# Four edits of an instruction order: the opening, the second half's x, the seam between the halves, the gate rows

## The chip, the cores and the metric

The kernel runs on one core of one Trainium2 chip. Five engines work side by side: TensorE (PE in the profile, its weight loads PEld), VectorE (DVE), ScalarE (ACT), GpSimd (POOL) and SyncE (SP), which issues nearly all DMAs. The metric is the device time of one execution in microseconds (us), median over runs; lower is better.

## The reference

One decoder block on x of 2048 tokens by 1024 channels, all in float32:

```python
mod = silu(c) @ w_ada + b_ada                       # shift, scale, gate: 1024 each
h = rms_norm(x, norm_w) * (1 + scale) + shift
a, b, g_conv, q, k, v, g_attn, m_conv, m_attn = split(h @ w_in)
u = silu(layer_norm(causal_conv31(a * sigmoid(b)))) * silu(g_conv)
y_conv = u @ w_conv_out
q, k = rope(rms_norm(q)), rope(rms_norm(k))         # 12 heads of 128
o = softmax_merge(dilated_window_attention(q, k, v) for 3 dilations) * silu(g_attn)
y = sigmoid(m_conv) * y_conv + sigmoid(m_attn) * (o @ w_attn_out)
out = x + gate * (y @ w_out)
```

## The kernel before

**Products.** Every projection is done with each operand split into a high and a low part (`_hi`, `_lo`; weights `sh`, `sl`), three matmuls for one. 2 × 2 blocks of tokens and channels are multiplied in the manner of Strassen, with seven block products (A11, A12, A21, A22 and sums S1 to S4 of blocks, against weights B11 to B22 and sums T1 to T4); `xs`, `s_d` and `h_d` hold such sums and scaled blocks of x. A slot is the time of one such block product on PE, some 12 matmuls of 128 × 128 by 128 × 512, and the whole program is laid out slot by slot.

**Order.** The tokens are done in two halves. In the first half come V of two pairs of heads (`plain_quads`, slots 0 to 15), four plain query and key jobs of eight slots (`qkv_plain`, slots 16 to 47), then a chain of `qkv_quad` jobs with the attention units between them, then the gates (`gate_quad`, `ag_quad`) and the convolution's inputs (`ab_quad`); the second half has the same without the plain jobs. `at_slot(s, f, where)` puts a step at a slot; `run_agenda` calls the steps of a slot in the order "enter", "load", "act", "pe", "vec", "act2", the product, "tail", "store". PE always runs in this written order. DVE, ACT, POOL and SP do so from the start of each half to a few slots behind its last attention unit; outside that, a scheduler orders them.

**DVE's spare work.** Steps of the convolution (`conv_todo`; tiles `ce`, `cq`, `ca`) and 32 steps that scale and sum the second half's x (`later_todo`; tiles `xl11`, `xl12`, `xl21`, `xl22`, `xs3`, in four groups k = 0 to 3; `run_later`, L1483) are handed out at the end of each slot by an allowance: `credit` grows by PACE (by stage) plus `rest`, falls by the estimated DVE time of the slot, and while it is over 0.35 another step is issued. A group's tiles are loaded (`later_load`) when group k − 2 is done. One DVE line, L210, records nearly all of these operations.

**The opening.** x of the first half (tiles `hf0` to `hf7`, second index for 512 tokens) is squared, its sums go through `xm` to `xrow` (L1022) and `xst` (L1028), the roots come back as `xr`, and `x_scale` (L1039, L1041) scales hf. `angle_steps` (L1109 to L1113) work out the rotary angles on spare_hi and spare_lo, ACT takes sines (L1111), `table_turn` (L1118 ff.) writes the tables. `mod` (L1059) is the conditioning for blocks A12 and A22.

**The gate rows.** In the second half's gates, 16 tiles `wg` of rows of w_ada (the part for `gate`) are loaded (L1587) and added to `gate_sum` on DVE (`gate_add`), then two bias rows, then `gate_sum` goes through PE.

**Banks.** A product's PSUM bank (`pav`, `pcv`, `pcab`, `pag_mc_d` and so on) must be emptied by ACT or DVE into spare_hi or spare_lo before PE can use it again; `ut` and `cq` are the first steps of a convolution block behind `pcab` and `paab`. `rwk` and `rsk` are the row of norms for keys and its spread.

## Time and profile before

| | |
|---|---|
| three runs | 2352.3, 2357.51, 2354.8 us; median 2354.8 |
| profiled execution | 2360.98 us; span 2358.4 us |
| granted TensorE clock in it | 0.993 |
| DMA | 445.76 MB, mean 189 GB/s |
| matmuls | 11438 |
| DVE, POOL instructions | 2792, 866 |

In the rows of the timeline the first number is the start in us from the span's start, the second the duration; then engine, line, operation, output <- inputs, and in brackets the idle time of that engine just before it and what ended it. Rows that follow each other overlap a little, since an engine begins an operation before the last has ended. Buffer numbers are left out of the names there; a name with a number belongs to the order of the program.

### The profile page before, as it was taken

To read this page: it belongs to the slowest core of one execution; us is meant where nothing else is said; L and a number is where in the kernel's file an instruction comes from. 1 tells how busy PE (TensorE), PEld (TensorE's weight loads), DVE (VectorE), ACT (ScalarE), POOL (GpSimd) and SP (SyncE) were. 2 spreads that over 40 slices of the span, in tenths; PEclk is the share of its full clock that TensorE was granted. 3 is DMA by queue.
4 is the path that set the end of the run, shared out by engine and by line. 5 is a ranking of instruction groups with operands and counts; after the bars stand their busy time and mean duration, and the time that the engine had idled before them with its cause. 6 is when DMAs were issued, how large, how long until landed. Compare 5 with 4: busy or idle time off the path is not lost.

```text
span 2358.4 us, 34462 instructions
## 1 busy us (share of the span) xinstructions
PE 2290.8 (97%) x11438; PEld 1868.6 (79%) x11438; DVE 1690.2 (72%) x2792; ACT 1120.8 (48%) x2291; POOL 1108.2 (47%) x866
## 2 busy tenths in 40 slices
PE   7999899999999999999999999999999999999999
PEld 4776688887878888787888887887888888888887
DVE  6668664566969789859746446799997957787544
ACT  5744455555644444654555545553444444332221
POOL 2345444545577789956433342445566630000221
PEclk9999999999999999999999999999999999999999
DMA  7567566665554455643666665655444579875553
GB/s 277 188 214 235 169 173 216 190 211 190 168 192 152 148 181 178 204 139 100 203 181 189 206 191 182 213 180 164 139 141 146 174 255 319 285 236 188 179 161 103
DMA packets 300942, 445.76 MB, mean 189 GB/s; under 512 B 28759, under 2 KB 132311, under 8 KB 300765
## 3 DMA queue, kind: packets, MB, share of 16 engines
q1 hardware_dynamic: 286648, 418.37, 55.8%
q10 hardware_dynamic: 14116, 25.20, 2.8%
q8 instruction: 90, 1.47, 0.3%
q14 instruction: 88, 0.71, 0.1%
HBM read 282.37 MB, written 161.09 MB: 188 GB/s over the span
## 4 chain that ended last, share of the span: by engine, by line
PE 50%; DVE 4%; DMA 2%; ACT 1%; issue 1%; POOL 0%; SPq 0%; ACTq 0%; DVEq 0%; POOLq 0%
PE yc L1710 8%; PE oa L1992 4%; PE ya L1710 4%; PE paab L345 3%; PE pak L345 3%; PE pav L345 3%; PE paq L345 2%; PE oc L1992 2%; PE pag_ma_d L345 2%; PE pcab L345 2%; PE pag_g_d L345 2%; PE po L945 2%; PE pcv L345 1%; DMA wg<-in_w_ada_dram 1%; PE pcq L345 1%; PE pck L345 1%
## 5 line engine op out<-in xcount | busy, mean ns | idle before, releaser
L282 POOL TENSOR_TENSOR slT<-wT,shT 128x512 fp32r<-128x512 f32 x172 | 232.8, 1354 | 283.9 <-ACT shT L281 270.6
L282 POOL TENSOR_TENSOR slB<-wB,shB 128x512 fp32r<-128x512 f32 x152 | 203.5, 1339 | 151.2 <-ACT shB L281 136.6
L281 ACT ACTIVATE shB<-wB 128x512 fp32r<-128x512 f32 x222 | 139.7, 630 | 167.5 <-issue 35.1
L282 POOL TENSOR_TENSOR slT<-wB,shT 128x512 fp32r<-128x512 f32 x98 | 131.8, 1350 | 148.1 <-ACT shT L281 120.6
L210 DVE SCALAR_TENSOR_TENSOR ce<-us,pair_taps,ce 128x512 f32<-128x512 f32 x240 | 180.9, 754 | 6.2
L210 DVE SCALAR_TENSOR_TENSOR ce<-ut,chan,ce 128x512 f32<-128x512 f32 x240 | 179.2, 747 | 0.5
L281 ACT ACTIVATE shT<-wT 128x512 fp32r<-128x512 f32 x176 | 110.4, 627 | 119.9 <-PE paab L345 21.2
L210 DVE SCALAR_TENSOR_TENSOR cq<-ut,chan,cq 128x512 f32<-128x512 f32 x208 | 155.2, 746 | 4.1 <-ACT cq L412 4.0
L210 DVE CUSTOM_DVE_ANT_0 sm<-ps,mask,rqq 128x256 f32<-128x256 f32 (+1 forms) x192 | 78.0, 443 | 93.0 <-PE ps L880 45.2
L276 POOL TENSOR_TENSOR wB<-wB,wB 128x512 f32<-128x512 f32 x80 | 111.2, 1391 | 47.2 <-DVE slB L210 44.1
L281 ACT ACTIVATE shT<-wB 128x512 fp32r<-128x512 f32 x120 | 75.2, 627 | 63.3 <-PE paab L345 30.7
L922 ACT ACTIVATE pT<-ptp 128x512 f32<-128x512 f32 (+2 forms) x84 | 44.8, 533 | 89.9 <-PE ptp L917 89.7
L139 POOL TENSOR_SCALAR stf<-stf 128x4 f32<-128x4 f32 x4 | 1.9, 473 | 179.9 <-DVE stf L1748 143.1
L945 PE MATMUL po<-v,pT 128*128 128x128 f32 x560 | 81.8, 277 | 3.0 <-ACT pT L922 2.8
L1920 ACT ACTIVATE yh<-yq 128x512 fp32r<-128x512 f32 x48 | 27.3, 623 | 120.4 <-POOL yq L1914 44.7
L945 PEld LDWEIGHTS po<-v,pT 128*128 128x128 f32 x560 | 75.1, 191 | 10.2 <-ACT pT L922 3.8
L210 DVE TENSOR_TENSOR slB<-wB,shB 128x512 fp32r<-128x512 f32 x70 | 54.9, 786 | 30.5 <-ACT shB L281 27.5
L902 ACT ACTIVATE sm<-sm,osb 128x256 f32<-128x256 f32 (+1 forms) x128 | 58.5, 463 | 4.2 <-DVE osb L210 4.2
L1911 POOL TENSOR_TENSOR ys<-yq 128x512 f32<-128x512 f32 x8 | 11.4, 1426 | 100.5 <-DMA yq<-y_d 88.8
L276 POOL TENSOR_TENSOR wT<-wB,wB 128x512 f32<-128x512 f32 x40 | 56.3, 1407 | 1.1
L917 PE MATMUL ptp<-ident,sm 128*128 128x128 f32 x332 | 52.3, 273 | 2.8 <-DVE stm L210 2.4
L622 POOL TENSOR_TENSOR slB_q<-wB_q,shB_q 128x512 fp32r<-128x512 f32 x16 | 29.5, 1846 | 54.3 <-ACT shB_q L621 49.7
(896 smaller groups left out, 7854.3 us busy)
## 6 DMA issues: line engine op xcount, KB each, us to landing
wB<-in_w_in_dram SPq DMA_DIRECT2D x262, 256.0 KB, 3.8
wT<-tT_d SPq DMA_DIRECT2D x136, 256.0 KB, 3.0
tT_d<-wB SPq DMA_DIRECT2D x102, 256.0 KB, 3.4
qk<-qk_d SPq DMA_DIRECT2D x96, 256.0 KB, 4.2
v_d<-vev SPq DMA_DIRECT2D x48, 256.0 KB, 3.4
qk_d<-spare_hi SPq DMA_DIRECT2D x48, 256.0 KB, 3.8
qk_d<-spare_lo SPq DMA_DIRECT2D x48, 256.0 KB, 4.1
v<-v_d SPq DMA_DIRECT2D x96, 128.0 KB, 3.9
```

Source lines behind the costliest of these rows:

```text
L210: return f(out, *args, **kw)
L276: nc.gpsimd.tensor_tensor(dst, x0, x1, op=ALU.subtract)
L281: nc.scalar.activation(h, q[name], AF.Copy)
L282: eng.tensor_tensor(l, q[name], h.bitcast(F32), op=ALU.subtract)
L345: nc.tensor.matmul(ps, x, y, start=(first and m == 0), stop=(last and m == 11), skip_group_check=True)
L622: nc.gpsimd.tensor_tensor(last[1], q[name], last[0].bitcast(F32), op=ALU.subtract)
L902: nc.scalar.activation(sm[:, a:z], sm[:, a:z], AF.Exp, scale=-1.0, bias=box["low"][i], accum_out=box["total"][i])
L917: nc.tensor.transpose(pt[:, c : c + P], box["sm"][:, c : c + P], ident)
L922: nc.scalar.activation(valid(pT), valid(pt), AF.Copy)
L945: nc.tensor.matmul(po[:, P * i : P * i + P], box["pT"][:, c : c + P], vt, start=(m == 0), stop=(m == count[i] - 1))
L1710: nc.tensor.matmul(pz, w, xx, start=(m == 0), stop=(m == len(terms) - 1))
L1992: nc.tensor.matmul(ps, y, w, start=(m == 0 and ps.name not in begun), stop=(m == 11 and not more), skip_group_check=True)
```

## The change

The diff is shown whole but for its headers.

```diff
-PACE, AFTER, AGAIN = (2.87, 3.15, 2.62, 2.85), (0.75, 0.1), 12
+PACE, AFTER, AGAIN = (2.87, 2.9, 2.62, 2.7), (1.0, 0.25), 12
...
     for k in range(4, KC):
-        at_slot(1, lambda k=k: x_scale(k, 0, pr), "act")
-    for s, count in ((0, 2), (1, 2), (2, 6)):
+        at_slot(2, lambda k=k: x_scale(k, 0, pr), "act")
+    for s, count in ((0, 2), (1, 1), (2, 5), (3, 2)):
         at_slot(s, lambda count=count: angle_steps(count))
...
         if k < 2 and later_todo[0][0] != k:
-            at_slot(s + 3, lambda: later_load(k + 2), "store")
-            later_from[k + 2] = s + 6
+            at_slot(s + 2, lambda: later_load(k + 2), "store")
+            later_from[k + 2] = s + 5
...
-        wa = aside["wg", i] = aside["gp"].tile([P, 512], F32, tag="wg", name=f"wg{i}")
+        wa = aside["wg", i] = aside["gp"].tile([P, 512], F32, tag="wg", name=f"wg{i}", bufs=2)
...
-        br = aside["gp"].tile([P, 512], F32, tag="wg", name=f"b_gate{i}")
+        br = aside["gp"].tile([P, 512], F32, tag="wg", name=f"b_gate{i}", bufs=2)
...
-        row = aside["gp"].tile([P, 512], F32, tag="wg", name=f"gate_out{i}")
+        row = aside["gp"].tile([P, 512], F32, tag="wg", name=f"gate_out{i}", bufs=2)
...
-    for i in range(2 * KC + 1):
-        if i:
-            at_slot(s + 2 * i, lambda i=i: gate_add(i - 1))
-        if i < 2 * KC:
-            at_slot(s + 2 * i, lambda i=i: gate_load(i))
+    for i in range(2 * KC):
+        at_slot(s + 2 * i, lambda i=i: gate_load(i), "load")
+        at_slot(s + 2 * i + 3, lambda i=i: gate_add(i))
...
-            kind, *job = jobs[i]
-            running[i] = kind(*job, columns[i][0])
+            running[i] = jobs[i][0](*jobs[i][1:], columns[i][0])
...
-        rest = AFTER[i >= half_jobs] if not waiting and s > busy_until[0] and stage % 2 else 0.0
-        credit = min(max(credit, -2.0) + PACE[stage] + rest - spent[0], 2.0)
+        rest = AFTER[i >= half_jobs] if not waiting and s > busy_until[0] and stage % 2 else 0.6 * (jobs[i][0] is qkv_plain)
+        credit = min(max(credit, -4.0) + PACE[stage] + rest - spent[0], 2.0)
```

In words: during plain query and key jobs the allowance grows by 0.6 per slot, its floor is −4 instead of −2, and the third and fourth group of x are loaded a slot sooner; the gate rows have two buffers, each row loaded at the start of its slot and added three slots later; in the opening four scalings go to slot 2 and the angle steps are dealt out anew. No instruction is added to PE or removed from it, and PE's order is the same.

On DVE, in the opening, the rows around the copy `xrow1` stood like this before (`hf2`, `hf3`: first 512 tokens):

```order
L1039 TENSOR_TENSOR hf2_0_176<-hf2_0_176,xr0_323 128x512 x2
L1039 TENSOR_TENSOR hf3_0_177<-hf3_0_177,xr0_323 128x512 x2
L1109 SCALAR_TENSOR_TENSOR spare_hi_169<-spare_lo_170,spare_hi_169 128x1024
L1109 SCALAR_TENSOR_TENSOR spare_hi_169<-spare_hi_169 128x1024
L1022 COPY xrow1_469<-xm1_415 128x128
L1028 TENSOR_SCALAR xst1_472<-xm1_415 128x4
L1109 SCALAR_TENSOR_TENSOR spare_hi_169<-spare_lo_170,spare_hi_169 128x1024
L1109 SCALAR_TENSOR_TENSOR spare_hi_169<-spare_hi_169 128x1024
L1110 TENSOR_SCALAR spare_hi_169<-spare_hi_169 128x1024
L1112 TENSOR_TENSOR spare_hi_169<-spare_hi_169 128x1024
L1113 TENSOR_SCALAR spare_hi_169<-spare_hi_169 128x1024
L1041 SCALAR_TENSOR_TENSOR hf0_1_178<-hf0_1_178,mod_140,xr1_495 128x512 x2
```
Here the scalings of hf2 and hf3 and two angle steps stand ahead of xrow1.

In the changed kernel the same stretch of DVE reads:

```order
L1109 SCALAR_TENSOR_TENSOR spare_hi_169<-spare_lo_170,spare_hi_169 128x1024
L1022 COPY xrow1_464<-xm1_411 128x128
L1028 TENSOR_SCALAR xst1_467<-xm1_411 128x4
L1039 TENSOR_TENSOR hf2_0_176<-hf2_0_176,xr0_323 128x512 x2
L1039 TENSOR_TENSOR hf3_0_177<-hf3_0_177,xr0_323 128x512 x2
L1109 SCALAR_TENSOR_TENSOR spare_hi_169<-spare_hi_169 128x1024
L1109 SCALAR_TENSOR_TENSOR spare_hi_169<-spare_lo_170,spare_hi_169 128x1024
L1109 SCALAR_TENSOR_TENSOR spare_hi_169<-spare_hi_169 128x1024
L1110 TENSOR_SCALAR spare_hi_169<-spare_hi_169 128x1024
L1041 SCALAR_TENSOR_TENSOR hf0_1_178<-hf0_1_178,mod_140,xr1_493 128x512 x2
L1085 SCALAR_TENSOR_TENSOR A21_lo_0_501<-hf0_1_178,mod_140,A21_hi_0_500 128x512
```
Now xrow1 and xst1 stand ahead of the four scalings; L1112 and L1113 follow behind four more rows, the last of them an A21_lo split.

On DVE, in the plain key jobs, ahead of the second use of `tmk` and `rwk`, the x steps stood like this before (`xl`, `xs3`: second half's x; the last digit is the group):

```order
L210 SCALAR_TENSOR_TENSOR xl212_1643<-xl212_1643,mod_140,rsx_1267 128x512
L210 TENSOR_TENSOR slB21_0_4096_1737<-wB21_0_4096_1652,shB21_0_4096_1736 128x512
L210 TENSOR_TENSOR S4_lo_0_1743<-s4_0_1684,S4_hi_0_1742 128x512
L210 SCALAR_TENSOR_TENSOR xl222_1645<-xl222_1645,mod_140,rsx_1267 128x512
L210 TENSOR_TENSOR S4_lo_0_1743<-s4_1_1705,S4_hi_0_1742 128x512
L210 TENSOR_TENSOR xs3_2_1809<-xl112_1639,xl212_1643 128x512
L210 SCALAR_TENSOR_TENSOR xl212_1643<-xl212_1643,edge_146,xl222_1645 128x512
L210 SCALAR_TENSOR_TENSOR xl112_1639<-xl212_1643,mod_140,xl112_1639 128x512
L210 SCALAR_TENSOR_TENSOR tmk0_1_00_1823<-spare_lo_170,hw_139,cos0_988 128x512
L210 SCALAR_TENSOR_TENSOR tmk0_1_01_1825<-spare_lo_170,hw_139,sin0_989 128x512
```
Group 2 is not finished where the rotation tmk begins.

In the changed kernel it reads there:

```order
L210 SCALAR_TENSOR_TENSOR xl112_1590<-xl212_1594,mod_140,xl112_1590 128x512
L210 TENSOR_TENSOR slB21_0_4096_1754<-wB21_0_4096_1657,shB21_0_4096_1753 128x512
L210 TENSOR_TENSOR S4_lo_0_1760<-s4_0_1697,S4_hi_0_1759 128x512
L210 SCALAR_TENSOR_TENSOR xl122_1592<-xl122_1592,mod_140,xl112_1590 128x512
L210 SCALAR_TENSOR_TENSOR xl113_1686<-xl113_1686,mod_140,rsx_1267 128x512
L210 SCALAR_TENSOR_TENSOR xl123_1688<-xl123_1688,mod_140,rsx_1267 128x512
L210 TENSOR_TENSOR S4_lo_0_1760<-s4_1_1721,S4_hi_0_1759 128x512
L210 SCALAR_TENSOR_TENSOR xl213_1690<-xl213_1690,mod_140,rsx_1267 128x512
L210 SCALAR_TENSOR_TENSOR xl223_1692<-xl223_1692,mod_140,rsx_1267 128x512
L210 TENSOR_TENSOR xs3_3_1824<-xl113_1686,xl213_1690 128x512
L210 SCALAR_TENSOR_TENSOR tmk0_1_00_1836<-spare_lo_170,hw_139,cos0_988 128x512
L210 SCALAR_TENSOR_TENSOR tmk0_1_01_1838<-spare_lo_170,hw_139,sin0_989 128x512
```
Group 2 is finished and five steps of group 3 are done ahead of tmk; over the whole stretch six more x steps stand ahead of the second rwk, and one fewer ahead of the third.

On DVE, at the seam between the halves, among the splits of the second half's first sums, the rows stood like this before (`ce`: convolution steps):

```order
L210 TENSOR_TENSOR S1_lo_1_9623<-landingS1_0_9512,S1_hi_1_9622 128x512
L210 SCALAR_TENSOR_TENSOR ce0_7_9230<-us0_7_9360,pair_taps_135,ce0_7_9230 128x512
L210 TENSOR_TENSOR S1_lo_1_9623<-landingS1_1_9514,S1_hi_1_9622 128x512
L210 TENSOR_TENSOR S1_lo_1_9623<-landingS1_2_9544,S1_hi_1_9622 128x512
L210 SCALAR_TENSOR_TENSOR ce0_7_9230<-us0_7_9360,pair_taps_135,ce0_7_9230 128x512
```
Two convolution steps stand between the S1 splits and the next.

In the changed kernel the same place reads:

```order
L210 TENSOR_TENSOR S2_lo_1_9537<-landingS2_2_9481,S2_hi_1_9536 128x512
L210 SCALAR_TENSOR_TENSOR ce0_7_9252<-us0_7_9386,pair_taps_135,ce0_7_9252 128x512 x3
L210 TENSOR_TENSOR S1_lo_1_9620<-landingS1_0_9511,S1_hi_1_9619 128x512
L210 TENSOR_TENSOR S1_lo_1_9620<-landingS1_1_9513,S1_hi_1_9619 128x512
L210 TENSOR_TENSOR S1_lo_1_9620<-landingS1_2_9542,S1_hi_1_9619 128x512
L210 TENSOR_TENSOR S3_lo_1_9683<-landingS3_0_9579,S3_hi_1_9682 128x512
L210 TENSOR_TENSOR S3_lo_1_9683<-landingS3_1_9581,S3_hi_1_9682 128x512
```
The two steps are gone from here; some twenty rows on, between the slT1 and slB22 splits, a run of five such steps has become one of seven.

On DVE, in the second half's gates, the adds of the rows stood like this around the eviction of `pcab` before:

```order
L210 SCALAR_TENSOR_TENSOR ce1_1_15844<-us1_1_15962,pair_taps_135,ce1_1_15844 128x512 x2
L210 SCALAR_TENSOR_TENSOR gate_sum_15996<-wg6_16301,sc_141,gate_sum_15996 128x512
L210 SCALAR_TENSOR_TENSOR ce1_1_15844<-us1_1_15962,pair_taps_135,ce1_1_15844 128x512 x3
L210 SCALAR_TENSOR_TENSOR gate_sum_15996<-wg7_16353,sc_141,gate_sum_15996 128x512
L210 SCALAR_TENSOR_TENSOR ce1_1_15844<-us1_1_15962,pair_taps_135,ce1_1_15844 128x512 x3
L210 TENSOR_TENSOR spare_lo_170<-spare_lo_170,pcab1_2_15757 128x512
L210 SCALAR_TENSOR_TENSOR gate_sum_15996<-wg8_16402,sc_141,gate_sum_15996 128x512
L210 SCALAR_TENSOR_TENSOR ce1_1_15844<-us1_1_15962,pair_taps_135,ce1_1_15844 128x512
L210 SCALAR_TENSOR_TENSOR ut1_2_15819<-spare_lo_170 128x2x256
L210 SCALAR_TENSOR_TENSOR ce1_1_15844<-us1_1_15962,pair_taps_135,ce1_1_15844 128x512
L210 SCALAR_TENSOR_TENSOR ut1_2_15819<-spare_lo_170,paab1_2_15689 128x2x256
L210 SCALAR_TENSOR_TENSOR ce1_1_15844<-us1_1_15962,pair_taps_135,ce1_1_15844 128x512
```
Eight row adds (wg0 to wg7) are done when pcab is evicted, with three convolution steps between two of them.

In the changed kernel it reads:

```order
L210 SCALAR_TENSOR_TENSOR gate_sum_15992<-wg12_16597,sc_141,gate_sum_15992 128x512
L210 SCALAR_TENSOR_TENSOR ce1_1_15864<-us1_1_15985,pair_taps_135,ce1_1_15864 128x512
L210 SCALAR_TENSOR_TENSOR gate_sum_15992<-wg13_16645,sc_141,gate_sum_15992 128x512
L210 SCALAR_TENSOR_TENSOR ce1_1_15864<-us1_1_15985,pair_taps_135,ce1_1_15864 128x512
L210 SCALAR_TENSOR_TENSOR gate_sum_15992<-wg14_16702,sc_141,gate_sum_15992 128x512
L210 SCALAR_TENSOR_TENSOR ce1_1_15864<-us1_1_15985,pair_taps_135,ce1_1_15864 128x512
L210 TENSOR_TENSOR spare_lo_170<-spare_lo_170,pcab1_2_15753 128x512
L210 SCALAR_TENSOR_TENSOR gate_sum_15992<-wg15_16749,sc_141,gate_sum_15992 128x512
L210 SCALAR_TENSOR_TENSOR ce1_1_15864<-us1_1_15985,pair_taps_135,ce1_1_15864 128x512
L210 TENSOR_TENSOR gate_sum_15992<-gate_sum_15992,b_gate0_16896 1x512
L210 SCALAR_TENSOR_TENSOR ut1_2_15819<-spare_lo_170 128x2x256
L210 SCALAR_TENSOR_TENSOR ut1_2_15819<-spare_lo_170,paab1_2_15684 128x2x256
```
Fifteen row adds are done when pcab is evicted, one convolution step stands between two of them, and a bias row stands ahead of ut.

## The prediction

> **What bounds the kernel now.** I read the page first (busy shares, the chain that ended last), then the table of stretches, then the timeline of the matmul engine (PE), stall by stall, and only then VectorE (DVE) around the four places that the change reaches.
>
> ```profile
> span 2358.4 us, 34462 instructions
> PE 2290.8 (97%) x11438; PEld 1868.6 (79%) x11438; DVE 1690.2 (72%) x2792; ACT 1120.8 (48%) x2291; POOL 1108.2 (47%) x866
> PE 50%; DVE 4%; DMA 2%; ACT 1%; issue 1%; POOL 0%; SPq 0%; ACTq 0%; DVEq 0%; POOLq 0%
> ```
>
> PE is the bound: 2358.4 − 2290.8 = 67.6 us of its span are idle, and a change that takes no matmul away can win only from these and from matmuls that run at half speed. In the stretches (length, busy time of PE, weight load, DVE, ACT, POOL with their counts, granted clock, DMA share, GB/s) the changed places differ from an undisturbed one, the last row:
>
> ```profile
> 0.00:50.00 50.00, 33.42 (x312) 22.07 (x316) 34.35 (x49) 22.16 (x34) 12.56 (x26) 0.93 0.81 302
> 200.00:250.00 50.00, 42.36 (x223) 31.84 (x223) 41.31 (x48) 18.63 (x30) 27.17 (x19) 0.93 0.62 201
> 1600.00:1650.00 50.00, 44.78 (x185) 36.15 (x184) 46.91 (x61) 19.00 (x33) 27.95 (x20) 0.93 0.52 169
> 1750.00:1800.00 50.00, 50.00 (x223) 41.38 (x222) 39.32 (x56) 23.72 (x40) 28.41 (x22) 1.00 0.48 158
> ```
>
> The stalls on PE at those places, the idle time in brackets with what ended it:
>
> ```profile
> 39.28 0.33 PE L1026 MATMUL xm<-ident,xrow 128*128 128x128 f32 x1 [2.99 <-DVE xrow L1022]
> 208.35 1.22 PE L737 MATMUL rsk<-rwk,pick 32*128 32x512 f32 x2 [3.18 <-DVE rwk L210]
> 260.24 0.50 PE L345 MATMUL pcv<-S_hi,shB 128*128 128x512 f32 x1 [1.07 <-DVE spare_hi L210]
> 265.89 1.19 PE L737 MATMUL rsk<-rwk,pick 32*128 32x512 f32 x2 [2.64 <-DVE rwk L210]
> 986.65 0.50 PE L345 MATMUL pav<-A_hi,shB 128*128 128x512 f32 x1 [2.98 <-ACT spare_hi L490]
> 1014.08 0.50 PE L345 MATMUL pcv<-S_hi,shB 128*128 128x512 f32 x1
> 1614.36 0.79 PE L345 MATMUL pag_mc_d<-S_hi,shT 128*128 128x512 f32 x1 [4.60 <-ACT spare_hi L360]
> 1614.95 0.63 PE L345 MATMUL pag_mc_d<-S_lo,shT 128*128 128x512 f32 x1
> 1642.54 0.50 PE L345 MATMUL pag_ma_d<-S_hi,shT 128*128 128x512 f32 x1 [0.61 <-ACT spare_lo L360]
> ```
>
> After the stalls of 2.64, 2.99, 3.18 and 4.60 us some ten matmuls run slow: they show 0.63 (row 1614.95) where an undisturbed one shows 0.40 (row 57.35 below), and ten times 0.23 is 2.3 us; read from the starts of the rows it is 1.7 to 2.9 each time. After the 2.98 at 986.65 none does. So a stall of this kind is worth its length plus up to 2.9. All that the change touches comes to about 25 us.
>
> PE's order does not change. DVE's does at four places, and only there: the two new PACE values, the new AFTER and the lower floor of the allowance move nothing in the first half's convolution, and little in the second's.
>
> **A, the opening.** xrow, which PE waits for (2.99), now stands on DVE ahead of four scalings of hf and one angle step; the angle steps L1112 and L1113 go behind the A21 splits.
>
> ```profile
> 34.16 2.47 DVE L1039 TENSOR_TENSOR hf<-hf,xr 128x512 f32<-128x512 f32 x4
> 38.95 0.28 DVE L1022 COPY xrow<-xm 128x128 f32<-128x128 f32 x1
> 45.22 1.23 DVE L1112 TENSOR_TENSOR spare_hi<-spare_hi 128x1024 f32<-128x1024 f32 x1 [2.22 <-ACT spare_hi L1111]
> 46.48 0.69 DVE L1113 TENSOR_SCALAR spare_hi<-spare_hi 128x1024 f32<-128x1024 f32 x1
> 53.32 2.03 ACT L1121 ACTIVATE ada_hi<-spare_hi 128x1024 f32<-128x1024 f32 x1
> 53.42 0.17 DVE L1059 TENSOR_TENSOR mod<-pt_ada,cols 128x8 f32<-128x8 f32 x1 [0.53 <-PE pt_ada L1056]
> 57.35 0.40 PE L345 MATMUL pC<-A_hi,shB_p 128*128 128x512 f32 x1
> ```
>
> xrow comes 2.47 us earlier, so the stall falls from 2.99 to about 0.5. But the four scalings are not gone; the same DVE work must be done before `mod`, on which A12, and so PE's slot from 57.35, depends. Between xrow and `mod` DVE idles for 2.22 + 0.53 = 2.75 us, so at most that can be won. The new order makes idle time of its own: DVE now stands at the foot of the chain PE → xrow → roots (about 1.4 with nothing ahead of it), and A21_lo waits for ACT, which has L1111 in front. I put these at 2.7, so `mod` stays near 53.3; ACT's table turn L1121 (2.03), which needs L1113, cannot start before that either, and A12_hi stands behind it. Bounds: −4.7 (stall 2.5 and the slow matmuls after it, if PE's lead lasts to 57.35) and +0.7 (L1113 later by its own length). I take 0, the end nearest to the row 57.35.
>
> **B, the second half's x.** With two of its groups loaded one slot sooner and 0.6 us per slot of extra allowance in the plain jobs, DVE does six more of these 32 steps before the second rwk, and one fewer before the third.
>
> ```profile
> L210 DVE SCALAR_TENSOR_TENSOR xl<-xl,mod,rsx x16: 739/746/1780, 138.6 to 224.1; 128x512 f32<-128x512 f32 x16
> 185.38 1.38 DVE L210 TENSOR_TENSOR S_lo<-s,S_hi 128x512 fp32r<-128x512 f32 x1 [1.94 <-ACT S_hi L193]
> 189.73 0.75 DVE L210 SCALAR_TENSOR_TENSOR xl<-xl,mod,xl 128x512 f32<-128x512 f32 x1 [0.47 <-DMA h_d<-xl]
> 207.63 0.67 DVE L210 TENSOR_TENSOR rwk<-pwk,edge 32x512 fp32r<-32x512 f32 x1
> 247.08 0.94 DVE L210 SCALAR_TENSOR_TENSOR xl<-xl,mod,xl 128x512 f32<-128x512 f32 x1
> ```
>
> Six steps by 0.70 (0.746 shown, less the overlap of neighbouring rows) are 4.2 us. DVE's idle time ahead of 207.63 that they can fill is 1.94 + 0.47 = 2.4. So rwk comes 4.2 − 2.4 = 1.8 later, and the stall of 3.18 becomes 5.0. The step at 247.08 (0.94 shown, 0.87 without the overlap) leaves the stretch in which DVE has no idle time before spare_hi (stall 1.07) and rwk (2.64): the first shrinks by 0.87, the second keeps its size because PE and DVE both come earlier. Net 1.8 − 0.9 = +0.9, plus 0.2 for a longer slow run: +1.1. The moved stores (h_d, s_d on SP's queue) have two slots to land and hide. Bounds: −0.9 (all six steps hidden) and +3.5 (none hidden, 4.2 + 0.2 − 0.9).
>
> **C, the seam between the halves.** Two convolution steps leave the stretch ahead of the add that feeds ACT's L490, and stand behind it in a run of seven instead of five.
>
> ```profile
> 982.18 1.27 DVE L210 TENSOR_TENSOR spare_hi<-spare_hi,pcg_g_d 128x512 f32<-128x512 f32 x2
> 1005.50 3.91 DVE L210 SCALAR_TENSOR_TENSOR ce<-us,pair_taps,ce 128x512 f32<-128x512 f32 x5
> 1012.94 1.08 DVE L210 TENSOR_TENSOR spare_hi<-spare_hi,pcv 128x512 f32<-128x512 f32 x1
> ```
>
> Two steps are 1.3 to 1.6 (3.91/5 = 0.78 each): the add at 982.18 and PE's 986.65 come about 1.3 earlier. The eviction at 1012.94 ends at 1014.02, and PE's pcv starts at 1014.08, so it has 0.1 us to spare. PE would reach it 1.3 earlier, and DVE does the same work before it: the 1.3 is given back there. Net +0.2; bounds −1.4 and +0.7.
>
> **D, the gate rows.** Sixteen rows of w_ada are loaded and added on DVE; one buffer forces load, add, load.
>
> ```profile
>   DMA wg<-in_w_ada_dram: 5.1, 7
> L210 DVE SCALAR_TENSOR_TENSOR gate_sum<-wg,sc,gate_sum x14: 739/1004/1839, 1582.0 to 1642.1; 128x512 f32<-128x512 f32 x14
> 1586.75 1.84 DVE L210 SCALAR_TENSOR_TENSOR gate_sum<-wg,sc,gate_sum 128x512 f32<-128x512 f32 x1
> 1586.75 1.29 POOL L282 TENSOR_TENSOR slT<-wT,shT 128x512 fp32r<-128x512 f32 x1 [2.08 <-ACT shT L281]
> 1601.33 0.33 SPq L1587 DMA_DIRECT2D wg<-in_w_ada_dram  x1
> 1604.58 0.75 DVE L210 SCALAR_TENSOR_TENSOR gate_sum<-wg,sc,gate_sum 128x512 f32<-128x512 f32 x1 [1.03 <-DMA wg<-in_w_ada_dram]
> 1607.49 0.68 DVE L210 TENSOR_TENSOR spare_lo<-spare_lo,pcab 128x512 f32<-128x512 f32 x1
> 1612.59 0.69 ACT L412 ACTIVATE cq<-ut,chan 128x512 f32<-128x512 f32 x1 [3.23 <-DVE ut L210]
> 1613.73 0.57 ACT L360 ACTIVATE spare_hi<-pag_mc_d 128x512 f32<-128x512 f32 x1
> ```
>
> Here the 4.60 us stall comes about: PE's bank waits for ACT's L360, which stands behind L412, which waits for ut, which waits for the pcab add. After the change 15 gate adds stand ahead of that add, not 8, and five convolution steps fewer: 7 × 0.75 − 5 × 0.75 = +1.5. The waits of 5.1 us mostly go, since a row has its own buffer. But the adds come in pairs, and a buffer is free only when its add is done: load to add takes 3.25 (1601.33 to 1604.58), and with 0.1 to issue and an add of 1.0 a buffer turns in 4.4 us, two rows per turn, while the DVE work between two pairs (two adds, two steps) is 3.0 to 3.5. So rows wg10 to wg15 wait about 1 us per pair, 3 in all. 1.5 − (4 of the 5.1 that lie ahead of the pcab add) + 3 = +0.5 to +1.7, and two bias rows and one step less behind it bring ut to +0.4. Behind 1613 the remaining seven adds are gone, so PE's next stall, 0.61 at 1642.54, is taken as gone. Sum +0.4 + 0.0 − 0.6, rounded up to 0 since the row loads now sit two at a time in front of weight loads on SP. Bounds: −6.5 (stall below 2.6 with no slow matmuls, plus the 0.6) and +5 (every one of the 7 extra adds takes 1.84 beside POOL, as in row 1586.75: 7 × 1.84 − 5 × 0.75 − 4 = +5.1).
>
> For that last price the trace has both values: 0.75 for a gate add alone, and 1.84 for one that begins together with POOL's slT. [...] Taken for every add, it gives the upper bound; half of them beside POOL would make the sum +2.
>
> **The sum.** A 0, B +1.1, C +0.2, D 0 = +1.3 on the profiled execution's span of 2358.4 (2360.98 with what lies around it). That execution is 6.2 us over the median of the three runs, 2354.8, and the forecast is made for such a median: 2354.8 + 1.3 = 2356.1.
>
> **Rivals.** R1, faster: the two buffers take DVE's waits on rows away in full, ut is ready 2.5 us sooner, the stall of 4.60 falls to about 2.1 and is not followed by slow matmuls: −2.5 − 2.9 − 0.6 = −6.0, 2348.8 with nothing else, 2350 with B and C. For it: 5.1 us of waits in seven places; against: 7 more adds ahead of ut. [...] R2, also faster: the opening's lead lasts, −4.7 and up to −6.0 with other parts hidden: 2350. Against it: DVE's 2.75 us of idle time are all there is. [...] R4: the moved steps fill idle time only, and nothing moves PE: 2354.8.
>
> **Chances.** Forecast 0.46, R4 0.10, R1 0.17, R2 0.12, R3 0.15. A difference under 0.2% (4.7 us) cannot be told from none here, so R1 and R2 count as faster at nine tenths, R3 as slower, and of the forecast's spread 0.01 and 0.02 reach over the bounds: faster 0.27, same 0.56, slower 0.17. The range 2348.5 to 2361 takes in R1 and R3 at their prices; the forecast's own is 2352 to 2359.
>
> **What would show it.** A: the stall at xm near 0.5, PE's pC slot still at about 57. B: the stall at the second rwk about 5.0. C: PE at pav earlier by 1.3, a new stall of about 1.5 at pcv some 28 us later. D: the stall at pag_mc_d within 1 us of 4.6, DVE waiting for wg in pairs among the last six rows. Wrong it would be if the slow matmuls vanish after 1610 or after 36, or if the stall before pag_mc_d passes 7 us.

## The result, and the profile after

The changed kernel is slower: 2366.6 us median (2362.93 to 2371.21) against 2357.02 (2352.3 to 2359.21), a ratio of 1.0043 with a 95% interval of 1.0029 to 1.0057, so +10 us (+6.8 to +13.4). The forecast was 2356.1 and no measurable difference; 2366.6 lies above the range. Measured again beside the kernels below, the same change gave 1.0046 (1.0032 to 1.0059).

The page of the changed kernel, and the same four stretches as before (length, busy time of PE, weight load, DVE, ACT, POOL with counts, clock, DMA share, GB/s):

```profile
span 2363.7 us, 34466 instructions
PE 2293.8 (97%) x11438; PEld 1869.7 (79%) x11438; DVE 1686.1 (71%) x2792; ACT 1120.4 (47%) x2291; POOL 1102.7 (47%) x866
0.00:50.00 50.00, 36.79 (x334) 23.35 (x334) 34.13 (x49) 22.67 (x36) 11.60 (x26) 0.93 0.77 295
200.00:250.00 50.00, 39.30 (x198) 29.12 (x197) 41.27 (x48) 18.33 (x30) 25.85 (x17) 0.93 0.56 175
1600.00:1650.00 50.00, 45.24 (x192) 36.93 (x192) 46.82 (x70) 20.24 (x35) 27.46 (x20) 0.97 0.54 169
1750.00:1800.00 50.00, 50.00 (x220) 41.04 (x219) 44.37 (x64) 24.18 (x42) 27.61 (x22) 1.00 0.49 153
```

PE idles 69.9 us, 2.3 more than in the profiled execution of before, and does the same matmuls. From 200 to 250 us it is busy 3.1 us less; in the first 50 us it is busy 3.4 us more, which turns out to be lost again by 64 us. The two profiled spans lie only 5.3 us apart, since the one shown of before was a long one: 2360.98 us where the median is 2357.

PE's stalls at the places of the prediction, from the timeline:

```profile
36.99 0.33 PE L1026 MATMUL xm<-ident,xrow 128*128 128x128 f32 x1 [0.48 <-DVE xrow L1022]
190.19 0.43 PE L688 MATMUL pssk<-sqk,sel 128*32 128x128 f32 x8 [1.49 <-ACT sqk L669]
201.67 0.50 PE L345 MATMUL pcq<-S_hi,slT 128*128 128x512 f32 x1 [1.40 <-DVE slT L210]
214.85 1.22 PE L737 MATMUL rsk<-rwk,pick 32*128 32x512 f32 x2 [5.42 <-DVE rwk L210]
992.30 0.50 PE L345 MATMUL pav<-A_hi,shB 128*128 128x512 f32 x1 [3.73 <-ACT spare_hi L490]
1020.43 0.50 PE L345 MATMUL pcv<-S_hi,shB 128*128 128x512 f32 x1 [0.64 <-DVE spare_hi L210]
1554.09 0.41 PE L966 MATMUL pta<-ident,osb 128*128 128x128 f32 x2 [1.16 <-DVE stm L210]
1621.76 0.64 PE L345 MATMUL pag_mc_d<-S_hi,shT 128*128 128x512 f32 x1 [4.76 <-ACT spare_hi L360]
```

The stall at xrow is gone as forecast, the one at rsk is 5.42 (forecast 5.0), and four stand where there was none: pssk, pcq, pcv (0.64, forecast about 1.5) and, in the second half's attention, pta.

### The profile page after: what moved, and what is told of

It reads as the page before. It is cut to its first block, busy times and chain, and to the rows that moved or that the text cites. A ratio compares the mean times of both kernels' runs of the same rounds, so it can differ in the third digit from the quotient of the medians.

```text
span 2363.7 us, 34466 instructions
## 1 busy us (share of the span) xinstructions
PE 2293.8 (97%) x11438; PEld 1869.7 (79%) x11438; DVE 1686.1 (71%) x2792; ACT 1120.4 (47%) x2291; POOL 1102.7 (47%) x866
## 4 chain that ended last, share of the span: by engine, by line
PE 51%; DVE 3%; DMA 2%; ACT 1%; issue 1%; POOL 0%; SPq 0%; ACTq 0%; DVEq 0%; POOLq 0%
PE yc L1707 8%; PE oa L1989 4%; PE ya L1707 4%; PE paab L345 3%; PE pak L345 3%; PE pav L345 3%; PE paq L345 2%; PE oc L1989 2%; PE pag_ma_d L345 2%; PE pcab L345 2%; PE po L945 2%; PE pag_g_d L345 1%; PE pcv L345 1%; PE pck L345 1%; PE pcq L345 1%; PE pag_mc_d L345 1%
## 5 line engine op out<-in xcount | busy, mean ns | idle before, releaser
L276 POOL TENSOR_TENSOR wB<-wB,wT 128x512 f32<-128x512 f32 x40 | 54.8, 1369 | 0.0
```

The lines of the kernel that those rows point to most:

```text
L276: nc.gpsimd.tensor_tensor(dst, x0, x1, op=ALU.subtract)
```

## The experiments

**How they are read.** PE runs the same matmuls in the same order in every kernel, so the time between two given matmuls can be compared kernel by kernel, whatever went before. The table is worked out from the starts of PE's rows; a stretch is named by its place in the profile of before. "With" are the kernels that hold the part in question as the change has it, "without" those that keep it as before; kernels that have it in another form are in neither column. Neither are, in the fourth row, g4_scale (56.41) and g1_x_actq (56.77), where DVE's order there is the new one though the opening is not. Each kernel counts with its one profiled execution.

| stretch, part | with: lowest to highest, mean | without: lowest to highest, mean | cost |
|---|---|---|---|
| 36 to 64, opening | 30.03 to 30.09, 30.05 (5 kernels) | 27.42 to 28.19, 27.92 (11) | +2.1 |
| 150 to 240, second half's x | 95.71 to 97.57, 96.53 (5) | 89.37 to 92.11, 91.27 (9) | +5.3 |
| 960 to 1030, PACE and AFTER | 71.28 to 74.12, 72.77 (6) | 69.85 to 74.46, 71.78 (14) | +1.0 |
| 1545 to 1600, opening's effect there | 54.96 to 56.70, 55.98 (5) | 54.96 to 56.27, 55.15 (13) | +0.8 |
| 1600 to 1660, gate rows | 58.05 to 59.47, 58.48 (5) | 54.05 to 60.04, 56.53 (13) | +2.0 |

The sum is some +11, and the change as a whole measured +10. In the first, second and last row the costs stand clear of the spread (in the last but for two kernels with the old rows, 54.05 and 60.04); in the third the two ranges cover nearly the same times, so that +1.0 is not shown by them. How far chance goes can be seen from 530 to 700 us, where the order is the same in all kernels: the time went from 164.98 to 170.67.

**Four parts, each alone on the kernel before.**

```diff
e1_open
-        at_slot(1, lambda k=k: x_scale(k, 0, pr), "act")
-    for s, count in ((0, 2), (1, 2), (2, 6)):
+        at_slot(2, lambda k=k: x_scale(k, 0, pr), "act")
+    for s, count in ((0, 2), (1, 1), (2, 5), (3, 2)):
e2_x
-            at_slot(s + 3, lambda: later_load(k + 2), "store")
-            later_from[k + 2] = s + 6
+            at_slot(s + 2, lambda: later_load(k + 2), "store")
+            later_from[k + 2] = s + 5
-        rest = AFTER[...] if ... else 0.0
+        rest = AFTER[...] if ... else 0.6 * (jobs[i][0] is qkv_plain)
-        credit = min(max(credit, -2.0) ...
+        credit = min(max(credit, -4.0) ...
e3_pace
-PACE, AFTER, AGAIN = (2.87, 3.15, 2.62, 2.85), (0.75, 0.1), 12
+PACE, AFTER, AGAIN = (2.87, 2.9, 2.62, 2.7), (1.0, 0.25), 12
e4_gate
-        wa = aside["wg", i] = aside["gp"].tile([P, 512], F32, tag="wg", name=f"wg{i}")
+        wa = aside["wg", i] = aside["gp"].tile([P, 512], F32, tag="wg", name=f"wg{i}", bufs=2)
...
-    for i in range(2 * KC + 1):
...
+    for i in range(2 * KC):
+        at_slot(s + 2 * i, lambda i=i: gate_load(i), "load")
+        at_slot(s + 2 * i + 3, lambda i=i: gate_add(i))
```

> The opening alone (four scalings to slot 2, angle steps dealt out anew). Theory 1 (angle steps L1112 and L1113 now run beside POOL's slB_p and take about 2 us more, mod comes 2 us later; besides, the moved scalings shift the scheduler's order near 1550 us): +2 to +3.5 us, L1112 near 2.3 us and L1113 near 1.7 us instead of 1.23 and 0.69. Theory 2 (the opening is even, the loss arises only when all parts are together): within 1 us of before.

Measured: ratio 0.9997 (0.9986 to 1.0008), so -3.3 to +1.9 us: in the total theory 2 holds and theory 1's +2 is not reached. The stretch from 36 to 64 us shows the loss, 30.04, as in all kernels with this opening, and L1112 and L1113 took 2.31 and 1.65, as theory 1 has it. The profiled execution won it back at the gate rows, by the shortest stretch of all kernels, 54.05, with a stall of 0.93 before pag_mc_d; DVE's order there is that of before, so this was chance, and it does not explain the median of twelve executions. Why the total shows no loss stays open.

> The second half's x alone (loads one slot sooner, 0.6 per slot more in the plain jobs, floor -4). Theory 1 (an in-place x sum waits for its store to land, about 4.8 us, and SP's queue passes the delay on to the loads of s): +4 to +5 us, DVE idle 4 to 5 us on a store h_d<-xl near 172 us, the stall before the second rsk 5 us or more. Theory 3 (only the six steps' own time counts, as forecast): +1.1 us, no wait on h_d over 1 us.

Measured: 1.0012 (1.0002 to 1.0023), stretch 95.71. DVE waited 3.96 us for a store h_d<-xl, and the stall at rsk was 5.85. Theory 1 holds on the places; in time the interval reaches from +0.5 to +5.4, which theory 3's +1.1 lies in as well, but its "no wait on h_d over 1 us" is out.

> PACE and AFTER alone (two convolution steps moved behind the seam). Theory 1 (without the two steps the S splits queue behind POOL for just as long, so nothing is won ahead of the seam and 0.6 us is lost at pcv): +1 to +1.5 us. Theory 3 (won ahead, given back behind): +0.2 us, the stall before pav under 2 us.

Measured: 1.0005 (0.9994 to 1.0016). The stall before pav is 3.65, where ten of the 14 kernels that keep the old order had 3.63 to 4.83 and four 2.91 to 2.98; so nothing was won ahead of the seam. At pcv 1.97 us stand where there was nothing. Too small for the total to tell.

> The gate rows alone (two buffers, each row added three slots after its load). Theory 1 (as forecast, ut hardly later, the stall before pag_mc_d about 4.7 us, the one of 0.6 us behind it gone): -2 to 0 us. Rival (two buffers take the waits away): -6 us, stall under 2.6 us. Rival (adds packed beside POOL): +5 us.

Measured: 1.0000 (0.9989 to 1.0011). The stall before pag_mc_d was 3.99, so the rival of -6 is out; +5 is out too. The stretch took 58.16, 1.6 over the mean of the old rows.

**The change with one part left out, and whole.** `f1_no_x`, `f2_no_open` and `f3_no_gate` are the change without the lines of e2_x, e1_open and e4_gate; `f4_all` is the change.

```diff
f4_all, all of the above; f1_no_x without e2_x; f2_no_open without e1_open; f3_no_gate without e4_gate
+            kind, *job = jobs[i]
+            running[i] = kind(*job, columns[i][0])
-            running[i] = jobs[i][0](*jobs[i][1:], columns[i][0])
```

> The change without its part for the second half's x (opening, PACE and AFTER, gate rows stay). Additive theory (the sum of the single parts, -0.7 + 1.2 + 0): about +0.5 us. Theory of the gate region (with the new gate order a delay from upstream is no longer taken up in the old stall near 1610 us): +2 to +4 us. Theory 1 (the x part carries nearly half of the loss): 4 to 5 us faster than the whole change.

Measured: 1.0019 (1.0007 to 1.0032), +4.5 us. Against 1.0046 for the whole, the x part is the largest single loss, some 6 us.

> The change without the new opening. Additive theory: about +4 us (2.8 + 1.2 + 0). Theory of the gate region: +5 to +7 us, with the stall before pag_mc_d at 4 us or more.

Measured: 1.0039 (1.0027 to 1.0051), +9.2 us (+6.4 to +12.0), more than both theories have; stall before pag_mc_d 4.03.

> The change with the old gate rows (one buffer, load and add in turn). Additive theory: about +3.3 us, as the whole change. Theory of the gate region: +1 to +3 us, clearly below the whole change, with the stall before pag_mc_d near 1 to 2.3 us as in the single parts with the old gate rows.

Measured: 1.0031 (1.0021 to 1.0041), +7.3 us, again more than both have; stall before pag_mc_d 2.09.

> The whole change again (its one line that only unpacks a job is left as before; the order is the same), on the same chip as the kernels that leave a part out. Additive theory: +3.3 us (0.14%). Theory of the gate region: +7 to +10 us, as in the first comparison.

Measured: 1.0046 (1.0032 to 1.0059). The sum of the stretches, +11, gives 1.0047. The +3.3 read from the four totals is out; each of those has an interval of ±2.6 us, their sum one of about ±5, and they were read too finely. That the parts add up is not refuted by it: stretch by stretch they cost alone about what they cost together. In the total the theory of the gate region, +7 to +10, came nearer, but its place does not show it: in the stretch of the gate rows the old order took 56.32 in f3_no_gate, with the delays of all other parts ahead of it, and 56.53 on average.

**The opening: where the steps stand.**

```diff
g4_scale
-        at_slot(1, lambda k=k: x_scale(k, 0, pr), "act")
+        at_slot(2, lambda k=k: x_scale(k, 0, pr), "act")
g2_open_fill
-    for k in range(4, KC):
-        at_slot(1, lambda k=k: x_scale(k, 0, pr), "act")
-    for s, count in ((0, 2), (1, 2), (2, 6)):
+    for s, count in ((0, 2), (1, 2), (2, 4)):
         at_slot(s, lambda count=count: angle_steps(count))
+    for k in range(4, KC):
+        at_slot(2, lambda k=k: x_scale(k, 0, pr))
+    at_slot(2, lambda: angle_steps(2))
```

> The opening with only the four scalings moved, the angle steps as before. Theory 1: the stall before xm near 0.5 us, L1112 and L1113 at 1.23 and 0.69 us, the stretch from 36 to 64 us at 27.5 to 28.2 us (no gain, since the work ahead of mod is the same, and no loss).

Measured in one execution: the stretch took 28.75, over the range expected and over the 27.42 to 28.19 of the old opening, L1112 and L1113 1.22 and 0.69. So the scalings alone gain nothing, and most of the loss belongs to the angle steps. Timelines, of the changed kernel (DVE, then POOL) and of g2_open_fill:

```profile
51.37 2.30 DVE L1112 TENSOR_TENSOR spare_hi<-spare_hi 128x1024 f32<-128x1024 f32 x1
53.71 1.66 DVE L1113 TENSOR_SCALAR spare_hi<-spare_hi 128x1024 f32<-128x1024 f32 x1
55.29 0.15 DVE L1059 TENSOR_TENSOR mod<-pt_ada,cols 128x8 f32<-128x8 f32 x1
51.27 3.54 POOL L327 TENSOR_TENSOR slB_p<-wB_p,shB_p 128x512 fp32r<-128x512 f32 x2 [12.59 <-ACT shB_p L326]
```

```profile
43.09 1.21 DVE L1112 TENSOR_TENSOR spare_hi<-spare_hi 128x1024 f32<-128x1024 f32 x1
44.34 0.69 DVE L1113 TENSOR_SCALAR spare_hi<-spare_hi 128x1024 f32<-128x1024 f32 x1
52.65 0.17 DVE L1059 TENSOR_TENSOR mod<-pt_ada,cols 128x8 f32<-128x8 f32 x1 [1.89 <-PE pt_ada L1056]
```

In the changed kernel both steps begin together with POOL's slB_p and take 1.07 and 0.97 us longer than at 45 us before; mod is 1.87 later than its 53.42. There `mod` waits for no PE, it follows L1113 at once; without the 2.04 us that the two steps lost it would stand at 53.25 (an estimate). In g2_open_fill POOL is idle beside them, its slB_p begins at 50.57, and they have their old lengths, 1.21 and 0.69.

> The opening in another order: the four scalings stand between L1110 and L1112, where DVE waited 2.2 us for ACT's sine, and the angle steps keep their slots. Theory 1 (the loss was L1112 and L1113 beside POOL): L1112 1.23 and L1113 0.69 us again, the stretch of PE products from 36 to 64 us (28.0 before, 30.05 with the new opening) falls to 27.3 to 28.0; time within 1 us of before or 1 us faster. Theory of DVE's idle time (filling 2.2 us wins it all): 26 us there, 2 us faster.

Measured: 0.9997 (0.9986 to 1.0009), stretch 26.26, below what theory 1 expected and near the 26 of the other theory, whose 2 us in the total did not come. PE's stall has moved from xrow (0.48) to xr (3.17), and the slow matmuls that follow the stall at xrow in the profile of before are missing. With the same opening two kernels below took 26.24 (h4_best) and 28.06 (i2_fill_load, with slow matmuls behind xr). So no gain is shown in the total; the 2.1 us of loss are gone.

**The gate rows: waiting or packing?**

```diff
g3_gate4, as e4_gate but
-bufs=2
+bufs=4
```

> The gate rows alone, with four buffers instead of two. If the 1.8 us lost with two buffers come from DVE waiting for rows: DVE's wait on wg under 1 us, the stall before pag_mc_d under 2 us, the stretch of products 1600 to 1660 us at 55 to 57 (56.7 on average with the old rows, 58.5 with two buffers). If they come from the seven more adds ahead of the pcab eviction: stall 4 us or more and 58 or more, waits or not.

Measured: 0.9994 (0.9982 to 1.0007). DVE's waits on rows, from the waits of DVE between 1570 and 1660 us, in the changed kernel and in g3_gate4 (total, times, longest):

```profile
DVE gate_sum L210 <- DMA wg<-in_w_ada_dram: 4.9, 7, 1.3
```

```profile
DVE gate_sum L210 <- DMA wg<-in_w_ada_dram: 0.9, 1, 0.9
```

The stretch falls to 56.57, that of the old rows, but the stall is 3.36, between the 0.93 to 2.40 of the old rows (the profile of before, 4.60, apart) and the 3.99 to 5.78 of two buffers. The other kernel with four buffers, h4_best below, has 57.83 and 3.38. So neither theory holds whole.

The traces show where the two differ. With four buffers all sixteen rows and both bias rows stand ahead of the pcab eviction, ten more than before, and yet it comes no later: counted from the same PE matmul (at 1561.66 in the profile of before) at 44.57 and 45.37 us, where the old rows had it at 43.34 to 44.83 (before, 45.82, apart) and two buffers at 46.48 to 48.27. DVE's idle time just before the row adds ahead of it was 1.0 to 1.2 us with four buffers, 2.1 to 3.7 with the old rows and 3.5 to 4.9 with two buffers. So with two buffers the eviction is late, by the waits and the seven more adds together. What is left with four buffers comes behind the eviction, from a ut step that took 1.71 instead of 0.68. The same happened in the profile of before; ut and POOL's slT there, and in e2_x, which has the old rows too:

```profile
1609.53 1.77 DVE L210 SCALAR_TENSOR_TENSOR ut<-spare_lo 128x512 f32<-128x512 f32 x1
1609.49 1.26 POOL L282 TENSOR_TENSOR slT<-wT,shT 128x512 fp32r<-128x512 f32 x1 [5.78 <-ACT shT L281]
```

```profile
1614.52 0.68 DVE L210 SCALAR_TENSOR_TENSOR ut<-spare_lo 128x512 f32<-128x512 f32 x1
1614.60 1.75 POOL L282 TENSOR_TENSOR slT<-wT,shT 128x512 fp32r<-128x512 f32 x1 [4.71 <-ACT shT L281]
```

In both, the one that begins first keeps its length (slT 1.26, ut 0.68), and the other takes longer: ut 1.77 for 0.68, slT 1.75 for 1.26. In the profile of before slT was first, by 0.04, and the eviction was 1.1 late; these two make the 4.60 of some 2.4.

**The x part: which half, and through which queue?** In the changed kernel, the timelines of DVE, ACT and SP's queue:

```profile
174.88 0.75 DVE L210 SCALAR_TENSOR_TENSOR xl<-xl,mod,xl 128x512 f32<-128x512 f32 x1 [4.80 <-DMA h_d<-xl]
186.84 0.63 ACT L193 ACTIVATE S_hi<-s 128x512 fp32r<-128x512 f32 x1 [5.15 <-DMA s<-s_d]
165.51 3.86 SPq L1442 DMA_DIRECT2D xl<-in_xt_dram  x4
169.46 0.85 SPq L1445 DMA_DIRECT2D h_d<-xl  x2
171.87 4.11 SPq L1445 DMA_DIRECT2D s_d<-xl  x3
176.07 1.86 SPq L271 DMA_DIRECT2D wB<-in_w_in_dram  x4
178.07 2.49 SPq L1442 DMA_DIRECT2D xl<-in_xt_dram  x4
180.67 0.37 SPq L1393 DMA_DIRECT2D s<-s_d  x1
```

An x step works in place on a tile whose store h_d is still under way. That store was issued at 169.46 or after, behind four x loads that themselves wait for older stores (1.8 us for an s_d). DVE stands for 4.80 us; the store s_d of the step's result stands on SP (the run from 171.87 takes 4.11); and behind it wait the weights wB and the loads of s (first half's S4), for which ACT idles 5.15. ACT's eviction and square come late, and PE waits at pssk. The transfers themselves are not slower: a load of s took 6.0 us from issue to landing in the kernel before, 5.0 to 5.9 in h2_x_load and h3_x_rest below, and 3.9 to 6.6 in e2_x and the changed kernel, as far as the traces have its landing. Each experiment on this has its first wB load, first s load, DVE's wait on h_d and its stretch in the table; in the kernel before they are 168.2, 173.4, 0.5 and 92.0.

| kernel | wB us | s us | DVE on h_d us | 150 to 240 |
|---|---|---|---|---|
| h2_x_load | 168.6 | 173.3 | 1.6 | 88.99 |
| h3_x_rest | 171.2 | 174.5 | 0 | 91.26 |
| e2_x | 173.2 | 178.0 | 4.0 | 95.71 |
| g1_x_actq | 168.7 | 182.2 | 0.2 | 99.76 |
| h1_x_sact | 173.2 | 179.6 | 4.0 | 97.61 |
| i1_x_searly | 174.6 | 177.5 | 5.4 | 97.58 |

```diff
g1_x_actq, as e2_x and
-        at_slot(slot_now[0] + 1, lambda: nc.sync.dma_start(dst, src), "store")
+        at_slot(slot_now[0] + 1, lambda: nc.scalar.dma_start(dst, src), "store")
h1_x_sact, as e2_x and
-        nc.sync.dma_start(parked[k], s4_d[k])
+        nc.scalar.dma_start(parked[k], s4_d[k])
h2_x_load, of e2_x the later_load and later_from lines alone
h3_x_rest, of e2_x the rest and credit lines alone
i1_x_searly, as e2_x and
-        at_slot(last_a21 - 1 + k, lambda k=k: s4_load(k), "load")
+        at_slot(last_a21 - 2 + k, lambda k=k: s4_load(k), "load")
```

> The x part alone, with the stores of the scaled x (h_d, s_d) issued on ACT's queue instead of SP's. Theory 1 (the delay comes from SP's queue in order: the store of xl12 stands behind others, DVE waits 4 to 5 us for it, and the loads of s stand behind the next store): DVE's wait on h_d falls under 1.5 us, ACT's wait on s under 2 us, the stretch of PE products that took 92.0 before and 95.7 with the x part (150 to 240 us) falls to 92.5 to 93.5. Theory 3 (the six steps' own time): stays at 95 or more with no wait on h_d.

Measured: 1.0021 (1.0006 to 1.0037). The wait on h_d went as expected, the time did not: now SP's x loads waited 13.6 us for the stores on the other queue, and s stood behind them. Theory 1, that the h_d wait is the cause by itself, falls.

> The x part alone, with only the four loads of s (the first half's S4, tile s from s4_d) issued on ACT's queue, so that they no longer stand behind the x loads and stores on SP's. If the order of SP's queue makes the x part slow: ACT's wait on s under 1.5 us, no PE stall over 0.5 us at pssk near 188 us, the stretch of PE products 150 to 240 us at 93 to 94.5 (96.5 on average with the x part, 91.6 without). If the transfers themselves are slow because eight others run at once: s still lands 5 us or more after its issue and ACT still waits 3 us or more, 95.5 or more.

Measured: 1.0021 (1.0010 to 1.0032). This did not take away what it meant to: the loads of s were issued no sooner, and ACT, whose queue they were on, stood 3.60 us in their place. Rows of SP's and ACT's queues in this kernel:

```profile
173.21 1.84 SPq L271 DMA_DIRECT2D wB<-in_w_in_dram  x4
179.55 0.34 ACTq L1393 DMA_DIRECT2D s<-s_d  x1
179.93 0.63 ACT L669 ACTIVATE sqk<-spare_lo 128x512 f32<-128x512 f32 x1 [3.60 <-DMA wB<-in_w_in_dram]
```

> Only the loads of the third and fourth x group one slot sooner, the allowance as before. If the bunch of loads and stores ahead of s is what costs: 92 to 93.5 in the stretch 150 to 240 us (the x steps hardly move). If the sooner loads alone do it: 95 or more.

Measured: 88.99, and 2350.35 us for one execution, below what either theory has. The sooner loads alone cost nothing.

> Only the larger allowance in the plain jobs and the lower floor, the loads of the x groups at their old slots. If the earlier x steps and their stores carry the cost: 94.5 to 97 in the stretch 150 to 240 us. If the loads do: 92 to 93.

Measured: 91.26, and 2357.81 us for one execution, again below both. The larger allowance alone costs nothing either, though it puts four of the six extra x steps ahead of the second rwk. So it is not mainly the steps' own DVE time, but the two edits together.

> The x part alone, with the four loads of s one slot earlier on SP's queue, so that the first stands ahead of the four x loads of the last group. If the late loads of s carry the loss (s issued at 178 us or later in every slow kernel, at 173 to 174.5 us in every even one): the first s issued by about 175 us, ACT's wait on s under 1.5 us, no stall over 0.5 us at pssk near 186 us, the stretch of PE products 150 to 240 us at 91 to 93. If the extra DVE steps and the wait on h_d carry it: 95 or more.

Measured: 1.0035 (1.0022 to 1.0049). The loads of s did not get to 175 us: wB, ahead of them, was late too, and ACT now waited 7.0 us for wB and 4.0 for s. The stretch took 97.58, as the other theory has it, but since s came no sooner this does not decide between the two.

```profile
173.37 0.75 DVE L210 SCALAR_TENSOR_TENSOR xl<-xl,mod,xl 128x512 f32<-128x512 f32 x1 [5.35 <-DMA h_d<-xl]
177.45 0.70 SPq L1393 DMA_DIRECT2D s<-s_d  x1
199.33 0.63 ACT L281 ACTIVATE shB<-wB 128x512 fp32r<-128x512 f32 x1 [5.21 <-DMA wB<-in_w_in_dram]
```

What the six show together: wherever the loads of s go out at 177 us or later the stretch takes 95.7 or more, and where they go out by 174.5 it takes 92 or less. No experiment brought them forward with both halves of the part in place, so that SP's queue is the whole cause stays likely, not shown.

**Combinations.**

```diff
h4_best = g2_open_fill + g3_gate4
i2_fill_load = g2_open_fill + h2_x_load
```

> The two edits that looked better than before, together: the four scalings between L1110 and L1112, and four buffers for the gate rows. Sum of the stretches: -1.8 us in the opening and 0 us at the gates, so -1 to -3 us against before (ratio 0.9987 to 0.9996); against the changed kernel 11 to 13 us less. Rival: the gate rows pack beside POOL and give the gain back, 0 us.

Measured: 1.0004 (0.9992 to 1.0017); the opening took 26.24, the gate stretch 57.83. The gain expected is not there in the total.

> The opening with the four scalings between L1110 and L1112, and the x groups loaded one slot sooner without the larger allowance. Sum of the stretches: -1.8 us in the opening, -1 to -3 us from 150 to 240 us (one look at the sooner loads showed 89.0, before 90.9 to 92.0): -2 to -5 us against before. Rival: the short stretch of that one look was chance, -1.8 us or less.

Measured: 2351.98 us against 2354.99, ratio 0.9985 (0.9974 to 0.9996), so 1 to 6 us faster than before. Its profile does not say where: the opening took 28.06 and the x stretch 92.16 there, both like before. Of the 15 intervals of these experiments it is the only one below 1, and it was measured once, so that the gain is not confirmed. The 88.99 of h2_x_load was likely chance: g2_open_fill, with the old x part, had 89.37.

## Why the prediction was wrong

**A, forecast 0, measured +2.1.** The first half was right: the stall at xrow fell to 0.48 and was not a gain. Wrong was "so `mod` stays near 53.3": I priced L1112 and L1113 at their old 1.23 and 0.69 in a place where POOL's slB_p runs, and there they took 2.30 and 1.66. With the old lengths `mod` would have come near 53.3, by the estimate above, so the 2.04 us make up the +2.1. I had used the row for that, 1.84 beside slT against 0.75, for the gate rows alone. What it is in slB_p that lengthens them, no run shows.

**B, forecast +1.1, measured +5.3.** The sum for rwk was fair (5.0 forecast, 5.42 measured; 4.6 on average with the part, from 2.32 to 5.85, and 2.6 without), but by luck of two errors: four of the six steps hide, as h3_x_rest shows, and "The moved stores (h_d, s_d on SP's queue) have two slots to land and hide" failed. This term was put at nothing. DVE stood 3.9 to 4.8 us for the store in the five kernels with the part, wB and s were issued late, and PE waited at pssk (1.49, 1.5 on average) and pcq (1.40, 0.8 on average), where it had not waited before. That the store, queued behind loads, held up everything behind it on SP is the likely reason, not shown, as said above. Of the +5.3, 4.0 are idle time of PE and 1.3 slower matmuls, for which the sum had 0.2. The count was off, too: between the second and the third rwk stand six x steps fewer (three for nine), not one.

**C, forecast +0.2, measured +1.0, not clear of chance.** "The add at 982.18 and PE's 986.65 come about 1.3 earlier" failed. DVE's timeline from the first of the last six splits to the add, with the first and the last of POOL's rows beside it, before (first and last of DVE's rows) and changed:

```profile
972.95 0.80 DVE L210 TENSOR_TENSOR S_lo<-landingS,S_hi 128x512 fp32r<-128x512 f32 x1
...
977.74 4.52 DVE L210 TENSOR_TENSOR S_lo<-landingS,S_hi 128x512 fp32r<-128x512 f32 x3
973.16 1.75 POOL L282 TENSOR_TENSOR slT<-wB,shT 128x512 fp32r<-128x512 f32 x1
...
981.67 1.75 POOL L282 TENSOR_TENSOR slB<-wB,shB 128x512 fp32r<-128x512 f32 x1
```

```profile
978.62 9.29 DVE L210 TENSOR_TENSOR S_lo<-landingS,S_hi 128x512 fp32r<-128x512 f32 x6
987.83 1.27 DVE L210 TENSOR_TENSOR spare_hi<-spare_hi,pcg_g_d 128x512 f32<-128x512 f32 x2
978.83 1.74 POOL L282 TENSOR_TENSOR slT<-wB,shT 128x512 fp32r<-128x512 f32 x1
...
987.32 1.73 POOL L282 TENSOR_TENSOR slB<-wB,shB 128x512 fp32r<-128x512 f32 x1
```

From the first split to the add it is 9.21 us now (978.62 to 987.83) and was 9.23 with the two steps in between (972.95 to 982.18): six splits alone take 1.55 each where one of them had taken 0.80. POOL's six operations beside them begin 1.7 us apart in both traces, and the add begins 0.51 after the sixth (981.67 and 987.32). I read this as the two engines taking turns, so that DVE's two steps had filled time that it otherwise spends waiting for POOL; that is not shown, since no run took POOL's operations away. The 2.98 I started from was short, too: most kernels have 3.6 to 3.9 there.

**D, forecast 0, measured +2.0.** The stall came out as forecast, 4.76, but by luck of two errors. One is the baseline. 4.60 in the one profile of before is far from what the old order does: 0.93 to 2.40 in 12 other kernels that keep it. The other is the term for DVE's waits, 4 of 5.1 us gone and 3 come back: ahead of the eviction they were 3.5 in the profile of before and 2.1 to 3.7 in the others, and 3.5 to 4.9 with two buffers, so they grew where they were to shrink by 1. The eviction came 1.4 us later than in the profile of before (47.26 for 45.82) and about 2.4 later than usual, where ut was put at +0.4. R1, which fed on that stall, had little to win. No run shows the +5.1 with which R3 makes the upper end of the range, 2361, every extra add as long as the 1.84 beside slT: the adds' mean fell from 1.15 to 0.92 (the add of 1.0 in D is the median, 1004 ns; now 752). And the working that gives +5.1 for all adds beside POOL gives +1.3 for half of them, not +2.

**A place missed.** "Only there" was wrong: the opening's scalings also shift the scheduler's order near 1550 us, where PE now waits 1.16 at pta, +0.8 on average. The new order alone does not make the stall: 1.16 in five of the seven kernels that have it, g4_scale with only the scalings among them, and none in e1_open and f4_all.

The sum of +1.3 should have been +11. The range ended at 2361 because each upper bound was taken alone; with +0.7, +3.5, +0.7 and +5 added they gave +9.9.

## What to carry to other kernels

A step moved on one engine is priced at its new neighbours' cost: look what the other engines do at that time (L1112 took 2.30 us beside POOL's slB_p and 1.21 with POOL idle). An in-place step on a tile that had just been stored waited for that store here (4.80 us), and the first load of s further back on the same queue went out at 180.67 us, where it had gone out at 173.4; two edits that are each harmless can be costly together (91.26 and 88.99 us alone, 95.71 with both). A stall in one profile is a sample: before building a term on it, look how it stands in another kernel with the same order at that place.

## What the runs showed of the hardware

Whether slow matmuls followed a stall was not told by its length. The same stall at the same place was followed by eleven matmuls at half speed in e4_gate and by none in e3_pace, where DVE's and PE's orders are the same:

```profile
265.97 1.19 PE L737 MATMUL rsk<-rwk,pick 32*128 32x512 f32 x2 [2.62 <-DVE rwk L210]
267.08 0.80 PE L345 MATMUL pav<-A_hi,shT 128*128 128x512 f32 x1
267.68 0.63 PE L345 MATMUL pav<-A_lo,shT 128*128 128x512 f32 x1
```

```profile
264.69 0.70 PE L737 MATMUL rsk<-rwk,pick 32*128 32x512 f32 x2 [2.67 <-DVE rwk L210]
265.31 0.50 PE L345 MATMUL pav<-A_hi,shT 128*128 128x512 f32 x1
265.65 0.39 PE L345 MATMUL pav<-A_lo,shT 128*128 128x512 f32 x1
```

The granted clock from 268 to 272 us was 0.50 in e4_gate, and from 267 to 271 us 1.00 in e3_pace. Of the 20 kernels 18 show six or more slow matmuls after this stall (2.62 to 3.15 us long) and two none; after the stall of 3.73 before pav in the changed kernel there is none. The granted clock stays at 0.50 for 3.4 or 6.8 us each time, 7 times between the start and the end of the profile of before, 9 times in that of the changed kernel and 5 times in that of e3_pace. In the profile of before four such runs cost 1.7 to 2.9 us each, read from the starts of the rows; with 5 to 9 of them in an execution, the difference from one execution to the next can be several us (an estimate from these numbers). What else decides whether the clock falls, no run shows: it fell after 2.62 us in e4_gate and stayed at 1.00 after the 3.73 in the changed kernel.
